# Sliding-window attention steps inside a stream of products: 192 keys turned in place of 256, and steps taken at product ends

## The chip, the cores and the metric

The kernel runs on one core of one Trainium2 chip. The metric is the device time of one launch in microseconds (us); lower is better. Engines are named as in the profile: PE (matmul), PEld (its weight loads), ACT, DVE, POOL, and SP, which here mostly issues DMAs.

## The reference

One layer on x of 2048 rows by 1024 columns, float32. `u` is x scaled and shifted by a vector that depends on c; one wide projection of `u` gives everything else:

```
[q | k | v | attn_gate | pool_in | pool_gate | merge_a | merge_p] = u @ W_in
A = SlidingWindowGQA_with_sinks(q, k, v; T5 relative bias) * SiLU(attn_gate)   -> @ W_attn_proj
P = (GroupLinear(MultiScaleCausalPool(pool_in)) * pool_scale) * SiLU(pool_gate) -> @ W_pool_proj
y = (sigmoid(merge_a) * A + sigmoid(merge_p) * P) @ W_out * (1 + gate)
x = LayerNorm(alpha * x + y)
```

Attention has 16 query heads of 64 dimensions and 2 key/value heads, so that eight query heads share one. A query sees the 128 keys up to its own position, and each head has a sink, a logit that takes part in the softmax and adds no value. With blocks of 128 queries a block sees two blocks of keys, its own and the one before; in the first block of all, only its own.

## The kernel before

**Dense part.** Each float32 matrix is held as a rounded high part and the rest as a low part, and a product is high·high + high·low + low·high: three matmuls of 128 weights by 512 columns for each 128 of depth (`mm3`). The large products are done by a scheme with seven products in place of eight (`Quad`, products named B11, T1, T2, B21, T3, B22, T4), each of four depth tiles, so 12 matmuls. Seven products make a *quad*: one 128-column tile of the projection for half a sequence. Before a product, ACT casts its weights to the high part and DVE makes the low part (`w_set`); after it, `behind` evicts the sums from PSUM through ACT and DVE (such as `q_hi`, `q_lo`, `sig`).

**Order.** `plan` lays the products of all phases in one list, and `run` goes through it: at each product it emits the splits that are due (`before`), the loads, the product's matmuls, and the evictions. Every instruction is kept in the order in which the program emits it, engine by engine. The phases are g (start), o (13 quads, 91 products), e (pooling), for each half of the sequence, then the projections of the outputs.

**Attention** is an overlay on phase o (`overlay`). It has 64 steps in each half of the sequence: 8 pairs of heads j by 8 blocks b. `product` calls `beat()` after each depth tile, every three matmuls. A beat adds `rate` to a credit; when the credit reaches 1, one step is emitted on the spot, in the middle of a product if it so falls, and behind whatever dense work was emitted earlier. With `rate = (N + 3) / (n_slots - 48)`, n_slots = 364, that is a step every 4.7 beats. The first 12 beats of a phase are left out, and at the switch of the key head 8 and 5 more.

A step stands for a block of 128 queries of two heads, in two halves of 64 queries (`eo` in the code): 128 weights are two heads by 64 queries, with the high and the low part of the 64 dimensions one above the other. The values have the high part in 64 columns and the low part in 64 more, so that the two halves of `pv` are added at the end. Step n is a pipeline over four blocks:

- on PE: scores of block n (`lg`, four matmuls of 128x192, since the first 64 queries see keys 0 to 192 of the 256 and the others 64 to 256); transposes of block n−2 (`pt`, four of 128x128 into PSUM); values of block n−3 (`pv`, four matmuls of 128x256: two key halves by high and low part)
- on ACT: the two scalings of block n−1 by the reciprocal sum (`L`), the cast of the transposed probabilities to a high part (`pth`, 128x512), a copy of half the values (`o`), the two exponentials of block n (`L`, 128x193 with the sink)
- on DVE: the reciprocal, two fused adds of the bias with a minimum (`L<-lg,bt,nsink`), the low part (`ptl`), two sums of the values (`st`)
- on POOL: the sink into the next room (`L<-nsink`). The rooms for probabilities are zeroed once where keys are out of sight, so that all 256 can be turned.

In the first block of the first half (eight steps) only 128 keys exist, and the step has two transposes and two value matmuls.

The queries (`qs`), keys (`kk`), values (`vv`) and bias (`bt`) come by DMA from SP's queue out of DRAM, where the dense quads put them. `Pools` opens one pool of tiles for each phase. At the start of an overlay the keys are asked for, then the queries of two steps, the bias, the values.

Of the kernel before, what the change touches and what calls it, by code (L numbers as in the profile page):

```python
# [59 lines left out]
def kernel(  # L60
# [74 lines left out]
    k_d = dp.tile([2, P, 2, D], F32, name="k_d")  # L135
    v_d = dp.tile([2, P, 2, 2 * NB, P], F32, name="v_d")
    px_d = dp.tile([KT, P, S], F32, name="px_d")
# [31 lines left out]
    class Pools:  # L169
# [4 lines left out]
        def __enter__(self):  # L174
            self.stack = ExitStack()
            self.t = self.stack.enter_context(tc.tile_pool(name=self.name, bufs=1, reuse_waits="tile"))
# [388 lines left out]
    def kv_quad(s):  # L565
# [6 lines left out]
        def turn_v(ph, t, vt):  # L572
# [8 lines left out]
            q = sp if s else act  # L581
            defer(1, lambda: [q.dma_start(v_d[s, :, a, NB * t : NB * (t + 1)], v[:, a]) for a in range(2)])

# [207 lines left out]
    def overlay(ph, s, n_slots):  # L791

        tp = ph.t
        U = 2 * NB
        N = KT * U
        kvt, qts, bts = {}, {}, {}
        rooms = [tp.tile([P, 2 * 257 + 14], F32, tag=f"L{i}", bufs=1, name="L") for i in range(3)]
        for room in rooms:
            pool.memset(room[:, 1 + BAND : 1 + BAND + P], 0.0)
        marks, Es, Ls, pts, xs, pvs, outs, ags, kept = {}, {}, {}, {}, {}, {}, {}, {}, {}  # L800

        def load_k(kv):
            k = kvt["k"] = tp.tile([P, 2, D + s * P], F32R, tag="kk", bufs=1, name="kk")
            mine = slice(kv * HD, (kv + 1) * HD)
# [8 lines left out]

        def load_v(kv):
            v = kvt["v"] = tp.tile([P, 2 * NB + s, P], F32R, tag="vv", bufs=1, name="vv")
            if s:
                sp.dma_start(as32(v[:, 0]), v_d[0, :, kv, 2 * NB - 1])
            for a, b in ((0, 2), (2, 2 * NB)) if kv else ((0, 2 * NB),):
                sp.dma_start(as32(v[:, s + a : s + b]), v_d[s, :, kv, a:b])

        def load_q(h):
            if h >= N // 2:
                return
            j, t, c = h // NB, h // 2 % 2, h % 2
            q = qts[h] = tp.tile([P, 4, 2, HD], F32R, tag="qs", bufs=2, name="qs")
            for n in range(2):
                src = q_d[s, j, t, n, 4 * c : 4 * c + 4].rearrange("b (h d) c -> d (b h) c", h=2)
                sp.dma_start(as32(q[n * HD : (n + 1) * HD]).rearrange("p b h c -> p (b h) c"), src)

        def load_bias(j):  # L830
            if j >= KT:
                return
            bt = bts[j] = tp.tile([P, BAND], F32, tag="bt", bufs=2, name="bt")
            for h in range(2):
                e_src = e_rep[:, 2 * j + h, :]
                at_q = bass.AP(e_src.tensor, e_src.offset + P - 1, [[HEADS * ET - 1, HD], [1, BAND]])
                sp.dma_start(bt[h * HD : (h + 1) * HD], at_q)

        def new_l(n):
            if n < N:  # L840
                j, k0 = n // U, k0_of(n)
                room = Ls[n] = rooms[n % 3]
                marks[n] = room[:, 2 * 257 : 2 * 257 + 2], room[:, 2 * 257 + 2 : 2 * 257 + 4]
                pool.tensor_copy(room[:, k0 : 2 * 257 : 2 * 257 - 1 - k0], nsink[:, j : j + 1].to_broadcast([P, 2]))

# [4 lines left out]
        def k0_of(n):  # L850
            return P if s == 0 and n % U == 0 else 0

        def values(n):
            k0 = k0_of(n)
            pv = pvs[n] = bank("pv")[:, 0 : 2 * P].rearrange("p (e q) -> p e q", e=2)
            pair = xs.pop(n)
            todo = [(hf, x) for hf in range(k0 // P, 2) for x in pair]
            for i, (hf, x) in enumerate(todo):
                mm(pv, kvt["v"][:, n % U + hf - 1 + s, :], x[:, hf], start=i == 0, stop=i == len(todo) - 1)

        def scores(n):
            b, q = n % U, qts[n // 2]
            lg = bank("lg").rearrange("p (e k) -> p e k", e=2)
# [14 lines left out]
        def transposes(n):  # L878
            L = Ls.pop(n)[:, 1 : 1 + 4 * P].rearrange("p (e k) -> p e k", e=2)
            pt = ps.tile([P, 2, 2, P], F32, tag="pt", bufs=1, name="pt")  # L880
# [23 lines left out]

        def step(n):
            lg = scores(n) if n < N else None
            pt = transposes(n - 2) if 0 <= n - 2 < N else None
            if n - 3 in xs:
                values(n - 3)
            if n - 1 in Es:  # L910
                E, sm = Es.pop(n - 1)
                dve.reciprocal(sm, sm)
                for eo in range(2):
                    k0, k1 = span_of(n - 1, eo)
                    x = E[:, 1 + 2 * P * eo + k0 : 1 + 2 * P * eo + k1]
                    act.activation(x, x, AF.Copy, scale=sm[:, eo : eo + 1])
            if pt is not None:
                h0 = k0_of(n - 2) // P
                hi = tp.tile([P, 2, 2, P], F32R, tag="pth", bufs=1, name="pth")
                lo = tp.tile([P, 2, 2, P], F32R, tag="ptl", bufs=1, name="ptl")  # L920
                xs[n - 2] = hi, lo
                act.copy(hi[:, h0:], pt[:, h0:])
            o2 = None
# [3 lines left out]
            if lg is not None:  # L927
                j, L = n // U, Ls[n]
                nm, sm = marks.pop(n)
                for eo in range(2):  # L930
                    k0, k1 = span_of(n, eo)
                    a, c = (1 + 2 * P * eo + k for k in (k0, k1))
                    dve.tensor_tensor_reduce(
                        L[:, a:c],
                        lg[:, eo, k0:k1],
# [6 lines left out]
                    )  # L942
                    with_sink = L[:, a : c + 1] if eo else L[:, a - 1 : c]
                    act.activation(
# [8 lines left out]
            if pt is not None:  # L953
                low(dve, lo[:, h0:], pt[:, h0:], hi[:, h0:])
            if o2 is not None:
# [11 lines left out]
                if bb == NB - 1:  # L967
                    defer(1, lambda: finish(jj, tt), True)
            if n < N and n % 2 == 0:
                load_q(n // 2 + 1)  # L970
# [7 lines left out]
        def beat():  # L978
            n, credit, rest = state
            if rest:  # L980
                state[2] -= 1
                return
            state[1] += rate
            if state[1] >= 1 and n < N + 3:
                step(n)
                state[0] += 1
                state[1] -= 1
                if n == N // 2 - 1:
                    load_k(1)
                    state[2] = 8  # L990
                if n == N // 2 + 2:
                    load_v(1)
                    state[2] = 5

        def leave():
            assert state[0] >= N, state
            while state[0] < N + 3:
                step(state[0])
                state[0] += 1

        load_k(0)
        load_q(0)
        load_bias(0)
        load_v(0)
        new_l(0)
# [733 lines left out]
```

## Time and profile before

| | us |
|---|---|
| median of 3 runs (lowest, highest) | 1689.68 (1688.29, 1690.58) |
| the profiled execution | 1685.7 |
| its span in the trace | 1683.8 |
| attention steps, first half | 159 to 472 |
| attention steps, second half | 732 to 1045 |

The clock granted to PE was 0.994 in the mean of this execution. In rows of the profile, a line such as `lg<-kk,qs 128*128 128x192 f32 x4` says that four matmuls wrote tile `lg` from tiles `kk` and `qs`, with weights of 128*128 and 128x192 moving. The start of an instruction can be read exactly; the durations of matmuls overlap, so that their price is the distance between starts. All engines' instructions show line 56, the helper that records them, so the tiles' names tell them apart. DMA issues by SP count as no busy time.

### The profile page before, as it was taken

To read this page: it belongs to the slowest core of one execution; us is meant where nothing else is said; L and a number is where in the kernel's file an instruction comes from. 1 tells how busy PE (TensorE), PEld (TensorE's weight loads), DVE (VectorE), ACT (ScalarE), POOL (GpSimd) and SP (SyncE) were. 2 spreads that over 40 slices of the span, in tenths; PEclk is the share of its full clock that TensorE was granted. 3 is DMA by queue.
4 is the path that set the end of the run, shared out by engine and by line. 5 is a ranking of instruction groups with operands and counts; after the bars stand their busy time and mean duration, and the time that the engine had idled before them with its cause. 6 is when DMAs were issued, how large, how long until landed. Compare 5 with 4: busy or idle time off the path is not lost. (4 is left out here: it accounts for less than half of the span.)

```text
span 1683.8 us, 24835 instructions
## 1 busy us (share of the span) xinstructions
PE 1654.8 (98%) x8146; PEld 1392.7 (83%) x8146; DVE 1164.9 (69%) x2161; ACT 962.7 (57%) x1944; POOL 588.4 (35%) x569
## 2 busy tenths in 40 slices
PE   8999999999999999999999999999999999999997
PEld 8888888888888888888888888888888888888885
DVE  6765666665648779546666666587867785878878
ACT  4555878788743346467877777344544343435453
POOL 3112454645552323323334244222332211114544
PEclk9899999999999999999999999999999999999999
DMA  9499777986557799875566553688968686777443
GB/s 349 137 306 302 197 233 203 265 219 202 173 181 234 267 316 309 274 188 163 172 179 202 151 171 127 222 281 304 347 207 303 230 309 203 264 259 266 151 151 124
DMA packets 340896, 384.77 MB, mean 229 GB/s; under 512 B 152200, under 2 KB 203424, under 8 KB 340640
## 3 DMA queue, kind: packets, MB, share of 16 engines
q1 hardware_dynamic: 334880, 376.99, 69.8%
q10 hardware_dynamic: 5856, 6.18, 1.1%
q8 instruction: 64, 1.05, 0.3%
q14 instruction: 64, 0.52, 0.1%
q0 software_dynamic: 32, 0.02, 0.0%
HBM read 238.91 MB, written 145.78 MB: 228 GB/s over the span
## 5 line engine op out<-in xcount | busy, mean ns | idle before, releaser
L56 PE MATMUL mm<-set_B,w_set 128*128 128x512 f32 x2664 | 651.5, 391 | 0.7 <-DVE w_set L56 0.7
L56 PEld LDWEIGHTS mm<-set_B,w_set 128*128 128x128 f32 x2664 | 496.1, 188 | 103.5 <-DVE w_set L56 1.5
L56 POOL TENSOR_TENSOR W<-W 128x512 f32<-128x512 f32 x185 | 268.0, 1459 | 584.2 <-DVE w_set L56 344.9
L56 PE MATMUL mm<-set_T,w_set 128*128 128x512 f32 x1896 | 463.7, 391 | 1.0 <-POOL w_set L56 0.7
L56 PEld LDWEIGHTS mm<-set_T,w_set 128*128 128x128 f32 x1896 | 349.7, 188 | 73.1 <-POOL w_set L56 1.9
L56 DVE TENSOR_TENSOR w_set<-W,w_set 128x1024 fp32r<-128x1024 f32 x197 | 255.5, 1297 | 107.6 <-ACT w_set L56 93.0
L56 ACT CAST w_set<-W 128x1024 fp32r<-128x1024 f32 x222 | 232.2, 1047 | 95.5 <-PE mm L56 55.6
L56 ACT ACTIVATE L<-L 128x193 f32<-128x193 f32 (+5 forms) x512 | 214.9, 446 | 99.5 <-DVE L L56 98.4
L56 PE MATMUL lg<-set_T,w_set 128*128 128x512 f32 x828 | 201.4, 391 | 1.4 <-DVE w_set L56 1.0
L56 PE MATMUL c<-set_T,w_set 128*128 128x512 f32 x828 | 200.8, 390 | 0.0
L56 PEld LDWEIGHTS lg<-set_T,w_set 128*128 128x128 f32 x828 | 155.1, 188 | 34.9 <-DVE w_set L56 1.8
L56 PEld LDWEIGHTS c<-set_T,w_set 128*128 128x128 f32 x828 | 155.5, 188 | 33.0 <-DVE w_set L56 0.8
L56 DVE TENSOR_TENSOR ptl<-pt,pth 128x512 fp32r<-128x512 f32 (+1 forms) x128 | 86.4, 675 | 117.5 <-ACT pth L56 117.5
L56 POOL TENSOR_TENSOR W<-W,A 128x512 f32<-128x512 f32 x41 | 58.1, 1418 | 271.1 <-DMA A<-in_win_dram 106.6
L56 DVE CUSTOM_DVE_ANT_0 L<-lg,bt,nsink 128x192 f32<-128x192 f32 (+2 forms) x256 | 93.6, 404 | 22.3 <-PE lg L56 21.7
L56 ACT ACTIVATE sig<-mm 128x512 f32<-128x512 f32 x76 | 45.5, 599 | 92.8 <-PE mm L56 89.8
L56 PEld LDWEIGHTS lg<-kk,qs 128*128 128x128 f32 x512 | 76.2, 190 | 15.7 <-issue 4.2
L56 POOL TENSOR_TENSOR w_set<-W,w_set 128x1024 fp32r<-128x1024 f32 x25 | 60.9, 2435 | 77.8 <-ACT w_set L56 69.4
L56 PE MATMUL pt<-ident,L 128*128 128x128 f32 x496 | 76.5, 275 | 5.7 <-DVE ptl L56 5.4
L56 PE MATMUL lg<-kk,qs 128*128 128x192 f32 (+2 forms) x512 | 75.8, 270 | 3.6 <-DMA qs<-q_d 2.9
L56 POOL TENSOR_TENSOR st<-st,ag 128x512 f32<-128x512 f32 x32 | 46.5, 1452 | 84.3 <-DVE st L56 78.5
L56 ACT CAST pth<-pt 128x512 fp32r<-128x512 f32 (+1 forms) x128 | 71.9, 562 | 6.4 <-PE pv L56 5.6
(211 smaller groups left out, 1905.9 us busy)
## 6 DMA issues: line engine op xcount, KB each, us to landing
W<-in_win_dram SPq DMA_DIRECT2D x40, 512.0 KB, 5.8
qs<-q_d SPq DMA_DIRECT2D x128, 128.0 KB, 4.3
sums_d<-W SPq DMA_DIRECT2D x62, 256.0 KB, 3.6
W<-sums_d SPq DMA_DIRECT2D x31, 512.0 KB, 3.6
ain_d<-st SPq DMA_DIRECT2D x56, 256.0 KB, 3.6
A<-in_win_dram SPq DMA_DIRECT2D x42, 256.0 KB, 5.5
q_d<-q_hi SPq DMA_DIRECT2D x32, 256.0 KB, 4.1
q_d<-q_lo SPq DMA_DIRECT2D x32, 256.0 KB, 3.9
```

Of the source, the lines that this page charges most:

```text
L56: return lambda *args, **kw: self.tc.keep_in_program_order(op(*args, **kw))
```

## The change

**Keys.** A query row sees at most 192 of the 256 keys of its two blocks. The step now turns and uses only these. The middle 128 keys are common to both halves of the queries; each half has 64 more, its *rest*. The step has two transposes of 128x128 (middle) and two that turn 64 columns (rests, `64x128` in the rows below); two value matmuls of 128x256 on the middle (high and low part, against `vv`), and two of 128x128 on the rests, where the high part stands in partitions 0 to 63 and the low part in 64 to 127 of one tile (`ptx`), against twins of the values with the same 64 keys in both halves (`vvl`, `vve`). The number of matmuls in an ordinary step is the same, 12; a first-block step has three transposes and three value matmuls (two and two before).

- ACT: the cast of 128x512 becomes one of 128x256 (`pth`) and one of 64x256 (`ptx`). DVE: the low part likewise. These tiles have two buffers each, one before.
- POOL: 124 copies of 64x128 make the twins (`twin_v`, in 32 of the 128 steps), and two small memsets belong to each first-block step. The memsets of the three rooms go.
- The values are kept in DRAM in another layout (`v_d`) and loaded shifted by 64 keys; query loads fetch four steps' worth in place of two.

**Steps.** `run` also calls `beat(2.0)` before a product's splits and after its matmuls, ahead of the evictions: a step that would come due within two beats is emitted there. `rate` is now 67/(364 − 55). The first 16 beats are left out in place of 12, and 8 and 8 at the switch of the key head. At the start the first half of the queries is asked for ahead of the keys; the values follow half-way through the rest.

The tiles of an overlay come from three pools in place of one, and the program is built with a smaller scratch for DMA descriptors (`dynamic_dma_scratch_size=2048`).

```diff
@@ run @@
+            if beat and p in before:
+                beat(2.0)
             for z, k, part in before.get(p, ()):
                 if not (z.opened and k in "FS"):
                     split_part(ph, z, k, part)
@@
                 product(getattr(q, acc), weights_of(q, kind, h), name, kind == "F", beat=beat)
+                if beat:
+                    beat(2.0)
@@ overlay @@
+        def twin_v(n):
+            b, v = n % U, as32(kvt["v"])
+            halves = slice(0, HD), slice(HD, P)
+            for name, of, shift in (("l", 0, 2), ("e", 1, 0)):
+                if name == "l" or not k0_of(n):
+                    for to in (of, 1 - of):
+                        pool.tensor_copy(kvt["v" + name][halves[to], b], v[halves[of], b + shift])
@@ values @@
-            pair = xs.pop(n)
-            todo = [(hf, x) for hf in range(k0 // P, 2) for x in pair]
-            for i, (hf, x) in enumerate(todo):
-                mm(pv, kvt["v"][:, n % U + hf - 1 + s, :], x[:, hf], start=i == 0, stop=i == len(todo) - 1)
+            hi, lo, rest = xs.pop(n)
+            b = n % U
+            todo = [(pv, kvt["v"][:, b + 1, :], x) for x in (hi, lo)]
+            for eo in range(2):
+                if eo or not k0_of(n):
+                    todo.append((pv[:, eo], kvt["vl" if eo else "ve"][:, b, :], rest[:, eo]))
+            for i, (to, v, x) in enumerate(todo):
+                mm(to, v, x, start=i == 0, stop=i == len(todo) - 1, skip_group_check=True)
@@ transposes @@
-            for hf in range(k0_of(n) // P, 2):
-                for eo in range(2):
-                    pe.transpose(pt[:, hf, eo, :], L[:, eo, hf * P : (hf + 1) * P], ident)
+            for eo in range(2):
+                mid = firsts[eo] + HD * (1 - eo)
+                pe.transpose(pt[:, eo], L[:, mid : mid + P], ident)
+            for eo in range(2):
+                if eo or not k0_of(n):
+                    rest = firsts[eo] + P * eo
+                    pe.transpose(pt[0:HD, 2 + eo], L[:, rest : rest + HD], ident)
@@ step @@
+            if (n - 2) % (N // 2) < U and n < N and n != N // 2 + 2:
+                twin_v(n - 2)
@@
-                act.copy(hi[:, h0:], pt[:, h0:])
+                act.copy(hi, pt[:, 0:2])
+                act.copy(rest[0:HD, e0:], pt[0:HD, 2 + e0 :])
@@
-                low(dve, lo[:, h0:], pt[:, h0:], hi[:, h0:])
+                low(dve, lo, pt[:, 0:2], hi)
+                low(dve, rest[HD:, e0:], pt[0:HD, 2 + e0 :], rest[0:HD, e0:])
@@ beat @@
-        state = [0, 0.0, 12]
-        rate = (N + 3) / (n_slots - 48.0)
+        state = [0, 0.0, 16]
+        rate = (N + 3) / (n_slots - 55.0)
@@
-            state[1] += rate
-            if state[1] >= 1 and n < N + 3:
+            if not early:
+                state[1] += rate
+            if state[1] + early * rate >= 1 and n < N + 3:
@@ start of the overlay @@
+        room_v()
+        load_q(0, (0,))
         load_k(0)
-        load_q(0)
         load_bias(0)
-        load_v(0)
```

What stands on PE in a quad of the second half, some 37 steps in, before (B21, T3 and B22 are the sets `set_B_68`, `set_T_411` and `set_B_459`):

```order
L56 MATMUL mm<-set_B_68,w_set 128x512 x9
L56 MATMUL mm<-set_T_411,w_set 128x512 x6
L56 MATMUL lg<-kk,qs 128x192 x4
L56 MATMUL pt<-ident,L 128x128 x4
L56 MATMUL pv<-pth,vv 128x256
L56 MATMUL pv<-ptl,vv 128x256
L56 MATMUL pv<-pth,vv 128x256
L56 MATMUL pv<-ptl,vv 128x256
L56 MATMUL mm<-set_T_411,w_set 128x512 x6
L56 MATMUL mm<-set_B_459,w_set 128x512 x9
```

and now, at the same place, from T3's product on:

```order
L56 MATMUL mm<-set_T_411,w_set 128x512 x12
L56 MATMUL lg<-kk,qs 128x192 x4
L56 MATMUL pt<-ident,L 128x128 x2
L56 MATMUL pt<-ident,L 64x128 x2
L56 MATMUL pv<-pth,vv 128x256
L56 MATMUL pv<-ptl,vv 128x256
L56 MATMUL pv<-ptx,vve 128x128
L56 MATMUL pv<-ptx,vvl 128x128
L56 MATMUL mm<-set_B_459,w_set 128x512 x12
L56 MATMUL lg<-kk,qs 128x192 x4
```

Steps moved from within a product to its end; in between stand 12 matmuls in runs of four to six steps, then 21, where before it was mostly 15 or 12.

ACT in a query quad of the second half, before (`L` of 128x192 the scalings, of 128x193 the exponentials; `q_hi` an eviction, `w_set` a split):

```order
L56 ACTIVATE q_hi<-p_8665 128x512
L56 ACTIVATE L<-L 128x192 x2
L56 CAST pth<-pt 128x512
L56 COPY o_8867<-pv 64x256
L56 ACTIVATE L<-L 128x193 x2
L56 ACTIVATE q_hi<-mm 128x512
L56 CAST w_set<-W 128x1024
L56 ACTIVATE L<-L 128x192 x2
L56 CAST pth<-pt 128x512
L56 COPY o_8926<-pv 64x256
L56 ACTIVATE L<-L 128x193 x2
L56 COPY mm<-mm 128x512
```

and now:

```order
L56 CAST w_set<-W 128x1024
L56 ACTIVATE L<-L 128x192 x2
L56 CAST pth<-pt 128x256
L56 CAST ptx<-pt 64x256
L56 COPY o_9358<-pv 64x256
L56 ACTIVATE L<-L 128x193 x2
L56 COPY mm<-mm 128x512
L56 ACTIVATE L<-L 128x192 x2
L56 CAST pth<-pt 128x256
L56 CAST ptx<-pt 64x256
L56 COPY o_9411<-pv 64x256
L56 ACTIVATE L<-L 128x193 x2
```

Between two steps' work on ACT stands less dense work at this place; the eviction `q_hi` that stood after the copy comes a step later.

POOL near the start of the first half, where the twins are made; each row of copies into `vvl` and `vve` is new, and they stand ahead of the sink copies and of the sums:

```order
L56 CAST vvl<-vv 64x128 x2
L56 CAST vve<-vv 64x128 x2
L56 COPY L<-nsink 128x2
L56 TENSOR_TENSOR ux<-ux 128x256
L56 TENSOR_TENSOR w_set<-W,w_set 128x1024
L56 CAST vvl<-vv 64x128 x2
L56 CAST vve<-vv 64x128 x2
L56 COPY L<-nsink 128x2
```

Before, the same stretch held only the sink copies and the sums, and one split (`w_set`) in the same place between them.

More of the change, by code (lines that the diff above doesn't have):

```diff
@@ L175, in __enter__, with room @@
             self.stack = ExitStack()
-            self.t = self.stack.enter_context(tc.tile_pool(name=self.name, bufs=1, reuse_waits="tile"))
+            def room(suffix=""):
+                return self.stack.enter_context(
+                    tc.tile_pool(name=self.name + suffix, bufs=1, reuse_waits="tile")
+                )
+            attends = "pv" in self.bufs
+            self.steps = room("_steps") if attends else None
+            self.t = room()
+            self.keys = room("_keys") if attends else None
             phase_ps["now"] = self.stack.enter_context(
@@ L791, in overlay @@
     def overlay(ph, s, n_slots):
-        tp = ph.t
+        tp = ph.steps
         U = 2 * NB
@@ L796, in overlay @@
         kvt, qts, bts = {}, {}, {}
[L797 to L800, printed above, removed]
+        firsts = 16 + BAND, 16
+        sinks_at = slice(15, 17 + 2 * BAND, 1 + 2 * BAND)
+        marks, Es, Ls, xs, pvs, outs, ags = {}, {}, {}, {}, {}, {}, {}
         def load_k(kv):
-            k = kvt["k"] = tp.tile([P, 2, D + s * P], F32R, tag="kk", bufs=1, name="kk")
+            k = kvt["k"] = ph.keys.tile([P, 2, D + s * P], F32R, tag="kk", bufs=1, name="kk")
             mine = slice(kv * HD, (kv + 1) * HD)
@@ new lines, in load_v @@
+        def load_v(kv, a, b):
+            v, first = as32(kvt["v"]), U * s
+            if a == 0 and s == 0:
+                pool.memset(v[0:HD, 1], 0.0)
+            for at, of, back in ((slice(HD, P), slice(0, HD), 1), (slice(0, HD), slice(HD, P), 2)):
+                a1 = a + back if a or not s else back - 1
+                sp.dma_start(v[at, a1 : b + back], v_d[of, kv, first + a1 - back : first + b])
+        def twin_v(n):
[5 more added lines that the diff above has]
+                        pool.tensor_copy(kvt["v" + name][halves[to], b], v[halves[of], b + shift])
@@ L832, in load_bias @@
                 return
[L833 removed]
+            bt = bts[j] = ph.keys.tile([P, BAND], F32, tag="bt", bufs=2, name="bt")
             for h in range(2):
@@ L841, in new_l @@
                 j, k0 = n // U, k0_of(n)
-                room = Ls[n] = rooms[n % 3]
-                marks[n] = room[:, 2 * 257 : 2 * 257 + 2], room[:, 2 * 257 + 2 : 2 * 257 + 4]
-                pool.tensor_copy(room[:, k0 : 2 * 257 : 2 * 257 - 1 - k0], nsink[:, j : j + 1].to_broadcast([P, 2]))
+                room = Ls[n] = tp.tile([P, 2 * BAND + 32], F32, tag="L", bufs=3, name="L")
+                marks[n] = tuple(room[:, 2 * BAND + i : 2 * BAND + i + 2] for i in (17, 19))
+                pool.tensor_copy(room[:, sinks_at], nsink[:, j : j + 1].to_broadcast([P, 2]))
+                if k0:
+                    for first in (firsts[0] + HD, firsts[1]):
+                        pool.memset(room[:, first : first + HD], BIG)
         def span_of(n, eo):
@@ L913, in step @@
                 for eo in range(2):
-                    k0, k1 = span_of(n - 1, eo)
-                    x = E[:, 1 + 2 * P * eo + k0 : 1 + 2 * P * eo + k1]
+                    a, c = seen(n - 1, eo)
+                    x = E[:, a:c]
                     act.activation(x, x, AF.Copy, scale=sm[:, eo : eo + 1])
             if pt is not None:
[L918 to L921, printed above, removed]
-                act.copy(hi[:, h0:], pt[:, h0:])
+                e0 = int(k0_of(n - 2) > 0)
+                hi, lo, rest = xs[n - 2] = [
+                    tp.tile([P, 2, P], F32R, tag=f"pt{z}", bufs=2, name=f"pt{z}") for z in "hlx"
+                ]
+                act.copy(hi, pt[:, 0:2])
+                act.copy(rest[0:HD, e0:], pt[0:HD, 2 + e0 :])
             o2 = None
```

67 lines of the change are left out of this document (40 added, 27 removed).

## The prediction

> **What bounds the kernel now.** I read the page's busy shares first, then the windows over the two stretches that hold the attention steps, since nothing outside them changes.
>
> ```profile
> PE 1654.8 (98%) x8146; PEld 1392.7 (83%) x8146; DVE 1164.9 (69%) x2161; ACT 962.7 (57%) x1944; POOL 588.4 (35%) x569
> ...
> 157.00:473.00 316.00, 310.44 (x1717) 265.78 (x1716) 198.45 (x597) 250.37 (x645) 158.38 (x179) 1.00 0.75 216
> 730.00:1046.00 316.00, 311.98 (x1746) 269.11 (x1745) 203.15 (x597) 244.17 (x629) 109.78 (x126) 1.00 0.59 169
> ```
>
> PE is busy for 310.4 and 312.0 of each 316 us. In the windows' order of columns ACT follows with 250 and 244, then DVE with 198 and 203. So the stretches can become shorter only by PE work that goes, or by the 4 to 6 us in which PE waits. Next, PE's waits over the whole trace and the two starts in the timeline (start, duration, idle before):
>
> ```profile
> PE pt L56 <- DVE ptl L56: 5.4, 14, 0.7
> PE lg L56 <- DMA qs<-q_d: 2.9, 2, 1.6
> PE lg L56 <- DVE L L56: 0.7, 2, 0.5
> ...
> 156.88 0.86 PE L56 MATMUL mm<-set_T,w_set 128*128 128x512 f32 x3
> 159.07 0.63 PE L56 MATMUL lg<-kk,qs 128*128 128x64 f32 x4 [1.34 <-DMA qs<-q_d]
> ...
> 729.66 0.86 PE L56 MATMUL mm<-set_T,w_set 128*128 128x512 f32 x3
> 732.13 0.66 PE L56 MATMUL lg<-kk,qs 128*128 128x192 f32 x4 [1.61 <-DMA qs<-q_d]
> ```
>
> Two waits on the first queries and some 14 on the low parts of the turned keys (ptl) are all that PE loses to attention: 9.0 us. What sets the second kind is seen in the groups of waits from 732 to 1045 us and in a stretch of the timeline:
>
> ```profile
> DVE ptl L56 <- ACT pth L56: 55.3, 63, 2.5
> ACT L L56 <- DVE L L56: 50.6, 34, 2.4
> DVE L L56 <- PE lg L56: 13.2, 16, 1.9
> ...
> 853.70 0.16 DVE L56 RECIPROCAL L<-L 128x2 f32<-128x2 f32 x1
> 854.66 0.56 ACT L56 CAST pth<-pt 128x512 fp32r<-128x512 f32 x1
> 855.32 0.59 PE L56 MATMUL lg<-kk,qs 128*128 128x192 f32 x4
> 856.32 0.19 ACT L56 ACTIVATION_READ_ACCUMULATOR L<-L 128x1 f32 x1
> 856.97 2.92 PE L56 MATMUL mm<-set_T,w_set 128*128 128x512 f32 x12
> 858.26 0.15 DVE L56 RECIPROCAL L<-L 128x2 f32<-128x2 f32 x1
> 859.73 0.59 PE L56 MATMUL lg<-kk,qs 128*128 128x192 f32 x4
> 860.56 0.66 PE L56 MATMUL pt<-ident,L 128*128 128x128 f32 x4 [0.25 <-DVE ptl L56]
> ```
>
> DVE and ACT mostly wait for each other (55 and 51 us) and seldom for PE's scores (13): within a step they are a chain. It runs from the reciprocal at 853.70 to the last exponential's sum, read by 856.51, so 2.8 us; then dense work until the next reciprocal at 858.26, 1.75 us. That is 4.56 us for one step, where PE takes 859.73 − 855.32 = 4.41 us, its waits included. Here ACT with DVE, not PE, sets the pace.
>
> **PE's share of the change.** A step has eight matmuls behind its four scores, before and after; 192 keys in place of 256 make four of them narrower and remove none. What width is worth is read from the starts of an ordinary step and of a first block, and from the transposes' groups:
>
> ```profile
> 249.76 0.59 PE L56 MATMUL lg<-kk,qs 128*128 128x192 f32 x4
> 250.19 0.60 PE L56 MATMUL pt<-ident,L 128*128 128x128 f32 x4
> 250.75 0.28 PE L56 MATMUL pv<-ptl,vv 128*128 128x256 f32 x1
> 250.86 0.28 PE L56 MATMUL pv<-pth,vv 128*128 128x256 f32 x1
> 250.98 0.28 PE L56 MATMUL pv<-ptl,vv 128*128 128x256 f32 x1
> 251.10 0.40 PE L56 MATMUL mm<-set_T,w_set 128*128 128x512 f32 x1
> ...
> 267.98 0.56 PE L56 MATMUL lg<-kk,qs 128*128 128x64 f32 x4
> 268.38 0.63 PE L56 MATMUL pt<-ident,L 128*128 128x128 f32 x4
> 269.32 0.40 PE L56 MATMUL mm<-set_T,w_set 128*128 128x512 f32 x1
> ...
> L56 PE MATMUL pt<-ident,L 128*128 128x128 f32 x496 | 76.5, 275 | 5.7 <-DVE ptl L56 5.4
> L56 PE MATMUL pt<-ident,mod 128*8 128x128 f32 x1 | 0.3, 271 | 0.0
> ```
>
> A step costs 251.10 − 249.76 = 1.34 us; three values of 256 columns fill 250.75 to 251.10, 117 ns each. Four scores of a first block, half of them 64 and half 128 wide, take 0.40 us, 100 ns each; four of 192 take 0.43. That step too lasts 269.32 − 267.98 = 1.34. So a 128-wide value is priced at 100 to 112 ns, and the two rests save 2 × 5 to 17 ns; I take 14 ns a matmul: 120 ordinary steps × 28 ns = −3.4 us at most, −1.2 at least. A transpose with 8 rows of weights is no shorter than one with 128 (271 and 275 ns), so the 64-wide ones save nothing. The eight first-block steps get one transpose and one value more: (1.34 − 0.43) / 8 = 114 ns each, 16 of them, = +1.8 us. Net −1.6 to +0.6; I take 0. If time did follow width, half of two transposes and two values would go, 2 × 57 + 2 × 59 ns over 120 steps = −28 us; with the values alone −14.
>
> The Trainium skill, "TensorE: Matmul & The Clock Gate", section "Back-to-back issue gap", gives about 81 ns for a matmul of 128 columns in a stream of weight loads and matmuls. By it the rests alone would save 2 × (117 − 81) × 120, an estimate of −8.6 us; the trace's 100 ns at 64 and 128 columns speaks against that.
>
> **The starts.** In the order of PE the first step stands nine matmuls later in both halves, and its queries' first half is issued ahead of the keys. Twelve matmuls from 856.97 to 859.73 take 2.76 us, so nine give 2.07. Start to start, with three matmuls at 0.23, the waits cost 159.07 − 156.88 − 0.69 = 1.5 and 732.13 − 729.66 − 0.69 = 1.8; both go: −3.3 us. What would be late next is the keys, which now stand behind the queries on SP and land about when those did: 0.3 us in hand at the second start. The value tiles, loaded half-way through the rest, are wanted three steps later; no row shows PE waiting for them. Fewer, larger query loads and the smaller scratch for descriptors I cost at nothing, since each load has more than one step's 4.4 us of lead.
>
> **The ACT and DVE work of a step.** Prices from the groups by form:
>
> ```profile
> L56 ACT CAST pth<-pt 128x512 fp32r<-128x512 f32 x120 | 69.0, 575 | 6.4 <-PE pv L56 5.6
> L56 ACT CAST pth<-pt 128x256 fp32r<-128x256 f32 x8 | 2.9, 357 | 0.0
> L56 DVE TENSOR_TENSOR ptl<-pt,pth 128x512 fp32r<-128x512 f32 x120 | 83.0, 692 | 113.0 <-ACT pth L56 113.0
> L56 DVE TENSOR_TENSOR ptl<-pt,pth 128x256 fp32r<-128x256 f32 x8 | 3.4, 425 | 4.5 <-ACT pth L56 4.5
> L56 POOL COPY L<-nsink 128x2 f32<-128x2 f32 x128 | 24.5, 210 | 2.1 <-ACT L L56 2.1
> L56 POOL TENSOR_TENSOR ux<-ux 128x256 f32<-128x256 f32 x64 | 55.4, 876 | 41.9 <-DMA wo_d<-ux 25.5 <-DVE ux L56 12.2 <-DMA u_d<-ux 3.4
> ```
>
> One cast of 575 ns becomes two of 357 (the 64-row one counted alike, since rows run side by side): +0.14 us a step on ACT. DVE's 692 becomes 2 × 425, +0.16, but the first low can begin beside ACT's second cast, so the chain grows by 0.14 to 0.3, from 2.8 to about 3.0 us. Behind each cast on ACT stand the value copy and both exponentials, and all of them come that much later.
>
> **Steps first.** A step due within two beats is now issued at a product's end, ahead of the eviction and the splits, so its chain no longer queues behind 1.75 us of dense work. That attacks the 5.4 + 0.7 us of ptl and L waits. In return steps stand 12 matmuls apart in runs of four to six and then 21, where before it was 15, 15, 15, 12. PE's period in a run is 2.76 + 1.34 = 4.10 us; the chain with its dense work needs 3.0 + 1.75 = 4.75, unless the eviction is put off to the 21-matmul gap. Over a quad the average, some 84 matmuls to six steps, hardly changes. At the switch of key head, where eight beats are left out, the gap grows; the higher rate makes it up. I assume half of the 6.1 us goes and the runs give back 2: −3 + 2 = −1.
>
> **POOL.** 124 copies of 64x128 (twins of the value tiles), four a step in 32 steps, and 16 memsets are added. A copy lies between the 0.21 us of a two-column one and half a 128x256 sum, 0.44: 0.8 to 1.8 us a step, of which I take 1.2. POOL is busy for 158 and 110 of 316 us, so most hides; those ahead of sums that splits need, or of the twin's own matmul, do not. I charge +0.5.
>
> **Sum.** −3.3 + 0 − 1 + 0.5 = −3.8, rounded to −4 us. The profiled execution took 1685.7 us (span 1683.8), 4.0 below the median 1689.68: by this sum it would be 1681.7, the median 1685.7. A measurement here tells 0.2%, 3.4 us, from no change.
>
> **Rivals.**
>
> *The chain becomes the bound (slower).* Place: runs of 12-matmul steps in the seven quads of each half whose evictions and splits load ACT (queries, gates, pool gate), T2 to B11. It decides once chain plus dense work exceeds 4.10 us for three steps running. At 4.75, each step in excess of what two buffers of pth and ptl absorb loses 0.65: one or two a quad, 14 quads, +9 to +18; less 3.3 for the starts, +6 to +14; I take +8, 1697.7. For it: the 4.56 above, and ACT at 79% on average. Against: the lighter quads catch up.
>
> *Width counts.* The bound above: −14 to −28; the values alone with the starts, about −18, 1671.7. Against it stands the first block's 1.34. The page's 81 ns would give less than half of that.
>
> *Steps first removes all.* −3.3 − 6.1 and the rests' −1.6: −11, 1678.7. For it: the chain waits behind dense work in the quoted stretch.
>
> *POOL's copies hold PE or DVE.* The sink copy and the split sums queue behind 1.2 us of twins, with a value's matmul after them:
>
> ```profile
> 784.49 1.89 DVE L56 TENSOR_TENSOR w_set<-W,w_set 128x1024 fp32r<-128x1024 f32 x1
> ...
> 852.56 1.23 DVE L56 TENSOR_TENSOR w_set<-W,w_set 128x1024 fp32r<-128x1024 f32 x1 [0.31 <-ACT w_set L56]
> ```
>
> The same split takes 1.23 us or 1.89. If a third of the 32 steps loses 0.4 to 0.6, it is +4 to +6; with the sum's rest, +2, 1691.7. The Trainium skill, "SBUF — State Buffer", section "SBUF: two separate sides", says that VectorE and GpSimd share one pair of ports as an exclusive lock; the 1.89 beside 1.23 would agree if POOL was running then, but the waits alone do not show it.
>
> **How the numbers follow.** Forecast 0.42 (its own range −8 to 0); chain bound 0.28; width 0.08; all removed 0.12; POOL 0.10. Below −3.4 us lie 0.27 of the forecast's 0.42, the 0.08 and the 0.12: faster 0.47. Within: 0.13 of the forecast, 0.05 of the chain's lower end, 0.06 of POOL's: same 0.24. The rest, 0.23 of the chain's, 0.04 of POOL's and 0.02 of the forecast's: slower 0.29. The range takes in the removal of all waits and the chain's middle, 1676 to 1700; left out are width (0.08) and the chain's upper end (about 0.09).
>
> **What would show it.** After the change no wait on qs at either start; a step of 1.34 us as before, with rest matmuls about 110 ns apart; two ACT casts near 0.36 us; fewer than 14 ptl waits. A step under 1.2 us would prove the width price wrong; ptl or L waits that add up to over 12 us, in the quads named, the chain's; waits of pv on POOL the copies'.

## The result, and the profile after

The changed kernel takes 1715.68 us (median of 4 runs, 1714.9 to 1718.19); the kernel before, beside it, 1689.87. The ratio is 1.016, with a 95% interval of 1.0145 to 1.0175: some 26 us slower. The forecast was 1685.7, in a range from 1676 to 1700. The profiled execution took 1718.19 us, 2.5 above its median, where that of before lay 4.2 below; so the spans, 1716.4 and 1683.8, differ by more than the medians.

The page's busy times, and PE's waits over the whole trace:

```profile
PE 1665.3 (97%) x8162; PEld 1396.9 (81%) x8162; DVE 1197.5 (70%) x2289; ACT 972.3 (57%) x2072; POOL 627.2 (37%) x705
...
PE pt L56 <- DVE ptx L56: 16.6, 21, 1.1
...
PE lg L56 <- DMA qs<-q_d: 3.4, 2, 2.8
PE pt L56 <- ACT L L56: 2.4, 3, 1.0
PE lg L56 <- DVE L L56: 2.2, 2, 1.3
```

The 5.4 us of waits on low parts have not shrunk but tripled, to 16.6, now on the rests' low part (`ptx`); the waits on queries are there again, at other steps. PE at an ordinary step, in the timeline:

```profile
1059.72 0.59 PE L56 MATMUL lg<-kk,qs 128*128 128x192 f32 x4
1060.14 0.60 PE L56 MATMUL pt<-ident,L 128*128 128x128 f32 x4
1060.50 0.36 PE L56 MATMUL pv<-pth,vv 128*128 128x256 f32 x1
1060.70 0.28 PE L56 MATMUL pv<-ptl,vv 128*128 128x256 f32 x1
1060.82 0.23 PE L56 MATMUL pv<-ptx,vve 128*128 128x128 f32 x1
1060.88 0.27 PE L56 MATMUL pv<-ptx,vvl 128*128 128x128 f32 x1
1060.99 0.90 PE L56 MATMUL mm<-set_B,w_set 128*128 128x512 f32 x3
```

Up to the next product's first matmul it looks 0.07 us shorter, 1060.99 − 1059.72 = 1.27, since the first narrow matmul takes 60 ns. But the matmul of 512 columns behind it pays most of that back: three of them span 0.90 us here, 0.86 elsewhere, and in the median over ordinary steps that do not stall the first of them lasts 284 ns to the next start, 232 before. To price a step with what it leaves behind, take the starts from the second product matmul ahead of it to the fourth after it, less five times 0.227 us. The median over 107 ordinary steps is 1.352 us before and 1.354 after. Fifteen steps that touch a first block went from 1.127 to 1.251.

The chain of a step on DVE and ACT, in the timeline of a late quad of the second half:

```profile
1017.96 0.16 DVE L56 RECIPROCAL L<-L 128x2 f32<-128x2 f32 x1
1018.92 0.35 ACT L56 CAST pth<-pt 128x256 fp32r<-128x256 f32 x1
1019.17 0.36 ACT L56 CAST ptx<-pt 64x256 fp32r<-64x256 f32 x1
1019.57 0.42 DVE L56 TENSOR_TENSOR ptl<-pt,pth 128x256 fp32r<-128x256 f32 x1 [0.79 <-ACT ptx L56]
1020.02 0.42 DVE L56 TENSOR_TENSOR ptx<-pt,ptx 64x256 fp32r<-64x256 f32 x1
1020.47 0.58 DVE L56 TENSOR_TENSOR st<-pv,o 64x128 f32<-64x128 f32 x2
1020.59 0.63 PE L56 MATMUL pt<-ident,L 128*128 128x128 f32 x4 [1.07 <-DVE ptx L56]
```

The first low part starts 40 ns behind the end of the *second* cast, not the first, and the three instructions of DVE stand 0.45 us apart, each after the one before has ended. From the reciprocal to the end of the value sums it is 1021.05 − 1017.96 = 3.09 us. In the stretch of before, whose reciprocal stood at 853.70, the low part and the sums were:

```profile
855.26 0.69 DVE L56 TENSOR_TENSOR ptl<-pt,pth 128x512 fp32r<-128x512 f32 x1 [0.73 <-ACT pth L56]
855.87 0.57 DVE L56 TENSOR_TENSOR st<-pv,o 64x128 f32<-64x128 f32 x2
```

so 856.44 − 853.70 = 2.74. (Over all steps the tenth percentile is 3.08 and 2.73; this figure is used below as the *DVE group* of a step.) In the changed kernel PE waits for the second low part: the transposes need the room in PSUM that it has just read.

**Where the 26 us are.** The spans of the two profiled executions differ by 32.6 us. Summed by the price above, all 134 steps take 184.6 us before and 212.3 after: +27.7. Of this, ordinary and first-block steps that stall are +23.7 (11.0 to 34.7 us over their price), the price of first-block steps +1.9, the first step of each half −3.4, the third step of each half +3.8 (mostly waits on queries) and the last steps of each half +1.7 (mostly waits on ACT's `sig`). Of the other 4.9 us, 3.8 lie ahead of the first step; the first experiment below, whose program is the same up to there, does not have them. The figures of 11.0 and 34.7 are called *stalls* below and given for the experiments. A stall costs more than the wait in the view: before, the rows of `ptl` and `L` add up to 6.1 us.

**The clock.** From 150 to 1100 us the clock granted to PE is 1.00 in these traces, except in spells at 0.50 that last 3.4 us, or two or three times that. Each stands behind or within waits of PE that add up to 1.7 us or more, such as a wait of 4.83 us on queries that ends at 172.6 in the first experiment:

```profile
171.00:178.00 7.00, 5.36 (x16) 4.54 (x17) 2.54 (x12) 4.83 (x16) 4.99 (x11) 0.51 1.08 288
```

The granted clock is the third number from the right. Not each such wait is followed by a spell: the 2.8 us on queries in the changed kernel are not. Matmuls take about twice as long in a spell (four scores 0.94 us to the next start in place of 0.43, in the run with the start alone), so that it costs up to half its length. The kernel before has none in that stretch and the changed one 3.4 us, so the 26 us are not a matter of the clock; but some of the experiments have up to 24 us, which belong to their times.

### The profile page after: what moved, and what is told of

Same layout as the page of the kernel before. It is cut to its first block, busy times and chain, and to the rows that moved or that the text cites. A ratio compares the mean times of both kernels' runs of the same rounds, so it can differ in the third digit from the quotient of the medians.

```text
span 1716.4 us, 25439 instructions
## 1 busy us (share of the span) xinstructions
PE 1665.3 (97%) x8162; PEld 1396.9 (81%) x8162; DVE 1197.5 (70%) x2289; ACT 972.3 (57%) x2072; POOL 627.2 (37%) x705
## 4 chain that ended last, share of the span: by engine, by line
PE 43%; DVE 4%; ACT 3%; issue 2%; DMA 0%; POOL 0%; DVEq 0%; ACTq 0%; POOLq 0%
PE mm L56 27%; PE lg L56 7%; PE c L56 6%; ACT L L56 1%; PE pt L56 1%; DVE wide L56 1%; PE pv L56 1%; DVE w_set L56 1%; ACT w_set L56 0%; DVE p L56 0%; DMA A<-y_d 0%; ACT pth L56 0%; ACT ptx L56 0%; DVE ptx L56 0%; DVE ptl L56 0%
## 5 line engine op out<-in xcount | busy, mean ns | idle before, releaser
L56 ACT ACTIVATE L<-L 128x193 f32<-128x193 f32 (+3 forms) x512 | 216.3, 448 | 93.2 <-DVE L L56 90.8
L56 DVE TENSOR_TENSOR ptl<-pt,pth 128x256 fp32r<-128x256 f32 x128 | 54.4, 425 | 88.5 <-ACT ptx L56 88.5
L56 PE MATMUL pt<-ident,L 128*128 128x128 f32 (+1 forms) x504 | 77.5, 276 | 21.9 <-DVE ptx L56 16.6
L56 DVE TENSOR_TENSOR st<-pv,o 64x128 f32<-64x128 f32 x256 | 72.6, 284 | 7.4 <-ACT o L56 1.7
L56 PEld LDWEIGHTS pt<-ident,L 128*128 128x128 f32 (+1 forms) x504 | 50.1, 126 | 27.1 <-issue 11.5
```

Source lines behind the costliest of these rows:

```text
L56: return lambda *args, **kw: self.tc.keep_in_program_order(op(*args, **kw))
```

## The experiments

A ratio is to the kernel before, run on the same chip, with its 95% interval. Stalls are those of ordinary and first-block steps, both halves together; 11.0 us before, 34.7 after. *Half clock* is the length of the spells at 0.50 from 150 to 1100 us; none before, 3.4 us after.

**Early beats taken out of the changed kernel.**

```diff
-            if beat and p in before:
-                beat(2.0)
...
-                if beat:
-                    beat(2.0)
```

> The changed kernel without the two early beats, so that a step is again emitted when its credit is full, in the middle of a product if need be; all else as changed. Theory of the runs (steps 12 matmuls apart outrun the chain on ACT and DVE): the waits of 37 us fall to about the 12 us of before, a step keeps its 1.28 us against 1.34, so about 1688 us (1684 to 1694). Theory of the rooms (POOL's sink copy now waits for the transposes, and holds POOL's queue): waits stay, 1705 us or more.

Measured: 1725.03 us, ratio 1.0224 (1.0203 to 1.0245), slower still. Stalls 34.9 us, waits on queries 8.1 us (one of 4.8), half clock 20.4 us. The theory of the runs falls: the stalls are there without runs of 12. What is slower than the changed kernel is not the stalls but the waits on queries (+4.7) and the half clock (17 us more, so up to 8.5).

**Fixed rooms for L in the changed kernel.**

```diff
+        rooms = [tp.tile([P, 2 * BAND + 32], F32, tag=f"L{i}", bufs=1, name="L") for i in range(3)]
-                room = Ls[n] = tp.tile([P, 2 * BAND + 32], F32, tag="L", bufs=3, name="L")
+                room = Ls[n] = rooms[n % 3]
```

> The changed kernel with three fixed rooms for L as before, in place of tiles taken from a pool; early steps stay. Theory of the rooms: the 72 us that POOL waits ahead of its sink copies fall to under 10, and the time falls by 8 to 20 us, to about 1700. Theory of the runs: the copies wait less, but PE's waits for ptx stay, and the time is within 4 us of the changed kernel's 1715.7.

Measured: 1713.62 us, ratio 1.0163 (1.0144 to 1.0182), stalls 32.2. The theory of the rooms falls too, and more than that: POOL's waits ahead of the sink copies did not go.

```profile
POOL L L56 <- PE pt L56: 58.0, 31, 5.5
```

So they do not come from the pool of rooms. They also cost little where they are: the run with one cast, below, has 89.4 us of them and stalls of only 6.6. What makes them was not looked into further.

**Early beats alone, on the kernel before** (the hunks of the first experiment added, and `beat(early)` with them).

> The kernel before with the early beats alone (rate, rests, keys, rooms as before). Theory of the runs: PE waits at the ends of the runs as in the changed kernel, +12 to +25 us over before, about 1708. Theory of the rooms: within 4 us of before's 1690, as its rooms are fixed.

Measured: 1696.64 us, ratio 1.0057 (1.0036 to 1.0079): +10, less than the runs would have it and more than the rooms. Stalls rose from 11.0 to 14.2; waits on queries from 2.9 to 4.7, half clock from none to 3.4.

**All three suspects out** (no early beats, fixed rooms, all first queries at the start).

> The changed kernel without early beats, with fixed rooms, and with both halves of the first queries asked for at the start (the second half behind the keys): what is left is the 192 keys, the twins on POOL and the later first step. Both theories: no added waits, 1.28 us a step, about 1682 us (1678 to 1688), that is below the kernel before. If it stays above 1695, a cause is missing from both: the split casts or the twins.

Measured: 1720.8 us, ratio 1.0201 (1.0182 to 1.0219). Both theories had said 1682. What was left, the rests, the twins and the faster pace, carries the loss. From here the theory is the *split chain*: two casts and two low parts in place of one each, in a chain that had no time to spare.

**Twins loaded by DMA**, so that POOL copies none.

```diff
-                        pool.tensor_copy(kvt["v" + name][halves[to], b], v[halves[of], b + shift])
+            for name, of, shift in (("l", slice(HD, P), 0), ("e", slice(0, HD), -1)):
+                z, a1 = as32(kvt["v" + name]), max(a, 1) if name == "e" and not s else a
+                for at in (slice(0, HD), slice(HD, P)):
+                    sp.dma_start(z[at, a1:b], v_d[of, kv, first + a1 + shift : first + b + shift])
```

> The changed kernel with the twin value tiles loaded by DMA in place of the 124 copies on POOL. Theory of POOL (the copies hold POOL's queue, the sink copies behind them and through them DVE and PE): 10 us or more faster than the changed kernel, below 1706. Theory of the split chain (two casts on ACT and two lows on DVE lengthen each step's chain by 0.25 to 0.35 us, and the chain was the bound already): within 4 us of 1715.

Measured: 1728.91 us, ratio 1.0242 (1.0225 to 1.0259). The stalls stay, 34.3, so the copies did not make them. With the added loads on SP's queue PE waits longer for queries, and half clock is 23.8 us:

```profile
PE pt L56 <- DVE ptx L56: 18.6, 21, 2.1
PE lg L56 <- DMA qs<-q_d: 12.0, 2, 6.9
```

**The rests' cast and low part left out** (their high and low parts stay zero; all matmuls stay).

```diff
-                act.copy(rest[0:HD, e0:], pt[0:HD, 2 + e0 :])
-                low(dve, rest[HD:, e0:], pt[0:HD, 2 + e0 :], rest[0:HD, e0:])
```

> The changed kernel without the second cast on ACT and the second low part on DVE: the rests' high and low parts are left at zero (their share of the values is left out), all matmuls, transposes and twins stay. Theory of the split chain: two instructions of about 0.36 and 0.42 us leave the chain in each of 120 steps; PE's 28 us of added waits go, and with the step's 1.28 us the time falls to 1685 or below (1675 to 1695). Theory of POOL: within 5 us of 1715.

Measured: 1687.33 us, ratio 0.9998 (0.9988 to 1.0009), 27 us below the changed kernel. The DVE group is 2.32 us, the stalls 6.5, and PE's waits for low parts have nearly gone:

```profile
PE pt L56 <- DVE ptl L56: 1.8, 5, 0.4
```

**The cast and the low part split, on the kernel before.**

```diff
-                act.copy(hi[:, h0:], pt[:, h0:])
+                for hf in range(h0, 2):
+                    act.copy(hi[:, hf], pt[:, hf])
```

and the low part likewise.

> The kernel before, with its cast of 128x512 and its low part of 128x512 each done in two instructions of 128x256, nothing else. Theory of the split chain: +0.14 us on ACT and +0.16 us on DVE in a chain that is already the bound give 0.25 to 0.3 us for each of 120 steps, +25 to +38 us over before, minus what the lighter quads absorb: +18 to +35. Theory of POOL or of the order of steps: within 4 us of before.

Measured: 1696.21 us, ratio 1.0048 (1.0031 to 1.0065): +8, well under what was expected. Stalls rise to some 17 us. The timeline shows a smaller growth of the chain:

```profile
1006.24 0.76 DVE L56 TENSOR_TENSOR ptl<-pt,pth 128x256 fp32r<-128x256 f32 x2 [1.02 <-ACT pth L56]
1006.91 0.57 DVE L56 TENSOR_TENSOR st<-pv,o 64x128 f32<-64x128 f32 x2
```

Here the two low parts run into each other: from the first to the value sums 0.67 us, against 0.61 with one low part and 0.90 in the changed kernel. The DVE group is 2.85, +0.12, not +0.35. In the changed program the second low part waits on a semaphore of DVE itself, which in this one it doesn't. That this wait is the cause isn't shown: the value sums behind `ptx` have no such wait and stand 0.45 us behind it all the same. `ptx` also differs in that it writes partitions 64 to 127 from inputs in 0 to 63; no run separates the two. This run also keeps the slower pace of before, 14.2 matmuls a step.

**One transpose for both rests, so one cast and one low part of 128x384** (values of the rests by four matmuls against tiles with zeros in the other half; fixed rooms).

```diff
-                    pe.transpose(pt[0:HD, 2 + eo], L[:, rest : rest + HD], ident)
+            pe.transpose(pt[:, 2], L[:, firsts[1] + P : firsts[1] + 2 * P], ident)
...
-                act.copy(hi, pt[:, 0:2])
-                act.copy(rest[0:HD, e0:], pt[0:HD, 2 + e0 :])
+                act.copy(hi, pt[:, 0:3])
```

> 192 keys and early steps as changed, but the two rests, which lie side by side in L, turned by one transpose into one block, so that one cast and one low part of 128x384 do; the rests' values by four matmuls of 128x128 against value tiles with zeros in the other half, loaded by DMA; fixed rooms. PE: one transpose less, two value matmuls more, about +0.06 us a step over the changed kernel, 1.34. Theory of the split chain: the chain is shorter than before's by about 0.25 us, so PE's waits fall below those of before, 1682 (1674 to 1692). Theory of the order of steps: the runs of 12 matmuls keep their waits, 1700 or more.

Measured: 1713.15 us, ratio 1.0153 (1.0138 to 1.0168). The time missed; the mechanism held. The DVE group is 2.49 us and the stalls 6.6 us, below those of before. Other things ate that: a step costs 1.46 us, +0.11 and not +0.06 (a narrow matmul is not cheaper than 110 ns), some 13 us over 120 steps; half clock is 13.6 us; and PE waits longer for queries:

```profile
PE lg L56 <- DMA qs<-q_d: 10.7, 2, 5.7
```

**The start alone, on the kernel before.**

```diff
-        load_k(0)
         load_q(0)
+        load_k(0)
...
-        state = [0, 0.0, 12]
+        state = [0, 0.0, 16]
```

> The kernel before with the start of the change alone: queries asked for ahead of the keys, first 16 beats left out in place of 12; keys, steps and rate as before. If the start does what the prediction said, both waits on the first queries go and the time falls by 3.3 us (2 to 4.5) below before. If SP's queue is what counts, the wait comes back at another load (a later query, the bias or the keys) and the time stays within 2 us of before.

Measured: 1694.56 us, ratio 1.0039 (1.0023 to 1.0055). The waits at the first step of each half went, −3.5 us, but two later loads are waited for, 2.1 us at 248 and this one:

```profile
824.17 1.14 PE L56 MATMUL lg<-kk,qs 128*128 128x192 f32 x4 [4.18 <-DMA qs<-q_d]
```

Behind it the clock is halved for 6.8 us: these four scores take 0.94 us to the next start, in place of 0.43.

**Only DVE's second low part left out** (the rests' low parts stay zero).

> The changed kernel without DVE's second low part (the rests' low parts stay zero, their share is left out); ACT's second cast stays. Theory of the split chain: the DVE group of a step falls from 3.08 to about 2.63 us; between the kernel with neither (2.32 us, 1687) and the changed one (3.08 us, 1716) that is about 1698 (1692 to 1704). If the second cast on ACT were what counts, it stays above 1708; if DVE's low alone, it reaches 1690 or less.

Measured: 1704.58 us, ratio 1.0101 (1.0078 to 1.0124), DVE group 2.58, stalls 22.4. ACT's cast and DVE's low part each carry a part, as the split chain says; the value missed the middle of the forecast by 7 us and lies just outside its range.

**A slower pace for the changed kernel**, `n_slots - 40.0` in the rate.

> The changed kernel with rate 67/(364 - 40) in place of 67/(364 - 55): a step falls due every 14.5 matmuls instead of 13.8, all else as changed. Theory of the split chain: each step has 0.16 us more, 120 of them, and the time falls by 6 to 15 us, to about 1705. If the pace does not matter (the runs between gaps stay 12 matmuls apart), within 4 us of the changed kernel.

Measured: 1703.24 us, ratio 1.0092 (1.0075 to 1.0109): −12, inside the range. Stalls 24.5, waits on queries 1.1 us, no half clock.

**The first queries' second half asked for sooner.**

```diff
+                if n == 0 and rest == 5:
+                    load_q(0, (1,))
```

> The changed kernel with the second half of the first queries asked for five beats before the first step and not right behind it. If the waits on it at the third step (2.8 and 0.6 us) are a late issue, they go: 2 to 4 us below the changed kernel, 1712 to 1714. If SP's queue is the limit, another load is late instead, and the time stays within 2 us of 1715.7.

Measured: 1717.2 us, ratio 1.0174 (1.0155 to 1.0192), no gain, though the waits on queries at the third steps are gone from its trace; stalls are some 2.4 us more, and all steps together only 1.5 us shorter.

**A still slower pace**, `n_slots - 30.0`.

> The changed kernel with rate 67/(364 - 30): a step falls due every 15.0 matmuls (13.8 as changed, 14.5 in the run before this). Theory of the split chain and its pace: another 0.11 us a step, -5 to -9 us from 1703, to about 1696. If what is left over before is a matter of loads, it stays within 3 us of 1703.

Measured: 1712.3 us, ratio 1.0141 (1.0119 to 1.0162), a miss. The stalls go on falling, to 20.5, but the last steps now end at 505 us, and the next phase waits for their stores:

```profile
513.03 2.36 DVE L56 TENSOR_TENSOR w_set<-W,w_set 128x1024 fp32r<-128x1024 f32 x2 [5.40 <-DMA ain_d<-st]
...
514.31 3.73 PE L56 MATMUL mm<-set_B,w_set 128*128 128x512 f32 x10 [2.66 <-DVE w_set L56]
```

PE's wait here is 2.7 us, and the ten matmuls behind it run in part at half clock. In all, half clock is 13.6 us against none in the run at `n_slots - 40.0`, which is up to 6.8 of the 9 us between the two runs.

**A slower pace for the kernel before**, `n_slots - 32.0`.

> The kernel before with rate 67/(364 - 32) in place of 67/(364 - 48): a step every 14.9 matmuls in place of 14.2. If its own 9 us of waits in steps come from the same chain, they fall by half and the time by 3 to 6 us, to about 1684. If its chain has time enough, within 2 us of before.

Measured: 1690.14 us, ratio 1.0019 (1.0006 to 1.0032): no gain. Waits on queries rose from 2.9 to 8.5 us, and 6.3 of these stand in ordinary and first-block steps; the other stalls went from 11 to about 10 only. So a slower pace takes little from the chain of this kernel, and the loads took it back.

**The same with early beats.**

> The same slow pace on the kernel before, with the early beats. If the runs of 12 matmuls that they make cost time of their own, +3 to +8 us over the run with the slow pace alone; if the early beats only hurt through the loads, within 3 us of it.

Measured: 1696.26 us, ratio 1.0043 (1.0029 to 1.0057), +4 over the slow pace alone by the ratios, +6 by the medians.

**The changed kernel at the slower pace without early beats.**

> The changed kernel at rate 67/(364 - 40), without the early beats, to stand beside 1703 with them. If early steps help a long chain (the dense work no longer stands ahead of it), +4 to +10 us; if their gain at the faster pace came from the loads, within 3 us.

Measured: 1716.58 us, ratio 1.0168 (1.0149 to 1.0188), 13 us above the run with them: stalls 30.2 against 24.5, waits on queries 6.8 against 1.1, half clock 10.2 us against none.

## Why the prediction was wrong

- **PE's price of the keys: right.** Net 0 was forecast; ordinary steps went from 1.352 to 1.354 us, and the first blocks' two matmuls cost 1.9 us (forecast 1.8). The estimate by the Trainium skill's 81 ns for a matmul of 128 columns ("TensorE: Matmul & The Clock Gate", "Back-to-back issue gap") does not hold here: two of them take 60 and 110 ns, and the matmul after them pays some 50 back.
- **The starts: right where they were looked at, and given back.** The first steps are 3.4 us shorter (3.3 forecast). But "Fewer, larger query loads" were costed at nothing, and with them the third steps wait for queries, 2.8 and 0.6 us. The start alone on the kernel before ended 5 us slower, by two late loads and the half clock behind one of them. How the order on SP's queue decides which load is late was not settled; the run with sooner queries shows only that moving one load does not help.
- **The step that failed: "the chain grows by 0.14 to 0.3", and no term for it in the sum.** The growth is 0.35 us in the DVE group, past the upper end. The forecast added whole durations, 0.14 for the casts and 0.16 for the low parts, and let part of the second go for overlap. In the rows above, from the first cast to the first low part is 0.65 us, where it was 0.60: the casts overlap and cost 0.05. From the first low part to the value sums is 0.90, where it was 0.61: the low parts cost 0.29, since they do not overlap with each other nor with the sums. The first low part does begin behind the second cast, not beside it. The larger fault is that the sum held −1 us for steps and nothing for the chain, though the prediction itself had read that ACT with DVE sets the pace. The runs tie the loss to the group's length at the changed kernel's pace: 2.32 us gives 6.5 us of stalls, 2.58 gives 22.4 and 3.08 gives 34.7, with the rate and the early beats the same. The run with one cast, 2.49 and 6.6, doesn't lie between them; its longer step on PE gives the chain 0.11 us more, so the length alone doesn't settle the stalls.
- **The pace** was told in the change (13.8 matmuls in place of 14.2) and had no term either. Given 0.16 us a step more, the changed kernel is 12 us faster, while the kernel before gains nothing from a slower pace. The faster pace was not tried on the kernel before, so what it costs without the longer chain is open.
- **The rival of the bound chain had the sign, and 8 us of the 26.** It also put the blame on the runs of 12 that early steps make. Without early beats the changed kernel is 11 to 13 us slower. At its own pace that is waits on queries and half clock, with stalls the same; at the slower pace 5.7 us of it are stalls. So only there do the runs show that early steps help a long chain. On the old keys the same beats cost 4 to 10.
- **POOL: small.** A twin copy takes 0.29 to 0.31 us (forecast 0.3, four at 1.2), and without the copies the stalls are the same. The split that took 1.89 us in place of 1.23 has a like in the changed kernel, with POOL's row beside it:

```profile
461.11 1.29 POOL L56 TENSOR_TENSOR st<-st 128x512 f32<-128x512 f32 x1
461.14 2.34 DVE L56 TENSOR_TENSOR w_set<-W,w_set 128x1024 fp32r<-128x1024 f32 x1 [0.25 <-ACT w_set L56]
```

The split is longer by about as much as the sum on POOL takes. That agrees with the exclusive lock on the ports shared by the two ("SBUF — State Buffer" of the Trainium skill, "SBUF: two separate sides"); no run isolates it.

None of the kernels beats the one before; the best with the whole computation and the new keys is the one with the slower pace, at 1.0092.

## What to carry to other kernels

Where two helper engines pass a small tile back and forth between the bound engine's visits, price a change by the length of that chain against the time between two visits, not by busy shares: here 0.35 us in each step became 24 us of stalls, with DVE busy for 69% of the time before; how much the faster pace had in that is not shown. Ask of two instructions in place of one whether they overlap, on their own engine and across, and count from start to start. Price a narrower matmul up to the first wide one behind it. And look at the granted clock before a difference between two runs is put down to the edit.

## What the runs showed of the hardware

- Two matmuls of 128 columns behind one of 256 start 60 and 110 ns apart, but the first 512-column one after them then lasts 284 ns to the next start, in place of 232 (medians): a step of 12 matmuls takes 1.35 us with either width.
- DVE instructions in a row overlap by some 80 ns in the kernel before split (two low parts of 128x256 and the sums behind them 0.67 us); in the changed kernel `ptl`, `ptx` and the sums stand 0.45 us apart, without overlap. A wait on DVE's own semaphore and other partitions for the output are what sets `ptx` apart; which counts is open.
- Loads on SP's queue can make PE wait for queries for 4 to 7 us: with 1 MB more of value tiles for each key head the waits went from 3.4 to 12.0 us, the longest 6.9, and with the start alone one of 4.2 came up. Which load is late was not worked out.
- Behind waits of PE that add up to 1.7 us or more the granted clock fell to 0.50 in many places, for 3.4, 6.8 or 10.2 us: after a wait of 4.2 us four scores took 0.94 us in place of 0.43. Not each such wait did it.
